# Self-attention of the sample streams in a hybrid streaming encoder: four 32-column tiles of the TensorE array, probabilities as the stationary operand

## The chip, the cores and the metric

The kernel runs on one core of one Trainium2 chip. The metric is the device time of one execution in microseconds (us), the median of three runs. A separate execution is recorded by the hardware profiler; every view of the profile below is of that one.

## The reference, cut to what matters

One inference layer of a chunk-causal encoder is computed for two groups of streams: a prompt of 2048 frames, and eight sample streams of 16 new frames each that carry 256 cached key and value rows. A layer is a mixer (banded attention with 8 heads of 64, beside a convolution module), a cross-attention into 256 memory tokens, and a feed-forward part, each with norms around it. The change touches only the banded attention of the samples:

```python
s = jnp.einsum("bqhd,bkhd->bhqk", qc, kc, preferred_element_type=jnp.float32) * scale + bias
s = jnp.where(valid[None, None, None, :], s, NEG_INF)
p = jax.nn.softmax(s, axis=-1)
return jnp.einsum("bhqk,bkhd->bqhd", p.astype(vc.dtype), vc)
```

For one sample the valid keys are its 256 cached rows and its own 16 new ones, 272 in all; there are 8 heads times 16 queries, so 128 rows of probabilities by 272 keys. All of it is float32.

## The kernel before, in words

The phases run one after the other in the program text: the memory keys and values, the input projection, the banded attention, the output projection of the mixer (`mixout`), cross-attention, gate and up, down. A planner of the language then orders the instructions of each engine by its own estimate of times and priorities, so that work of neighbouring phases and of different loop steps may stand mixed on an engine. Each engine then works off its list in that order.

`attention` walks over 128 units, one for each head and each block of 128 prompt queries. A unit makes scores (line 830), takes the softmax (lines 751 and 753), transposes the probabilities four steps later (line 847, four 128x128 transposes into a PSUM buffer of tag `t`, which ScalarE copies at line 848 and VectorE takes the remainder of at line 849) and multiplies by the values for four units at once (line 860, into the PSUM buffer of tag `o`, emptied at lines 864 and 866). The PSUM tags are `s` (two buffers of two banks), `t` (three buffers of one bank, given out in turn) and `o` (one buffer of one bank).

Beside the prompt runs one sample for each head: `sample(h)` is a generator, and the loop takes one step of it at every second unit (every unit in the first and last head, never at the first unit of a head). That gives seven steps in a head of the middle. The steps before the change:

- step 1 loads the sample's keys (line 758, on the SP queue) and values (lines 760 to 762, SP) and copies the new keys in (line 763, GpSimd). Steps 2 and 3 do nothing.
- step 4 fills `qb`, four blocks of 128 columns. Block c holds the queries of heads 2c and 2c+1, in 32 columns at the place 32c and zeros in the rest. Those zeros let four matmuls (line 776: 128 stationary columns, 272 moving) add up in one PSUM region to all 128 rows of scores. `qb` lies in two buffers of 128x640 words that are cleared once; because a block is written at a pitch of 160 words and read at one of 128, the place 32c comes about by itself. Softmax follows (lines 751, 753, 779, 780).
- step 5 transposes the probabilities in three blocks of 96, 96 and 80 keys (line 785, into a `t` buffer) and copies them to SBUF (lines 787 and 788, ScalarE), as `pp`.
- step 6 multiplies: for each of the four pairs of heads and each block of keys, the 128 value columns of the pair are stationary and the 32 probability columns move (line 794, 12 calls, into the `o` buffer). The result has channels on partitions, and VectorE copies the two halves that count into `attS` (lines 796 and 797). `mixout` reads `attS` for its first block.

A float32 matmul call of lines 776 and 794 stands in the trace as two weight loads and two matmuls: 4 calls a sample as 8 records at line 776, 12 calls as 24 at line 794. A transpose is one record a call.

Of the kernel before, what the change touches and what calls it, by code (L numbers as in the profile page):

```python
# [8 lines left out]
F32 = mybir.dt.float32  # L9
# [8 lines left out]
P = 128  # L18
# [12 lines left out]
DEC_S = 16  # L31
# [109 lines left out]
class Build:  # L141
# [591 lines left out]
    def attention(self):  # L733
        nc, A = self.nc, self.A
        sbF, sbR, ps, fa, fb = self.sbF, self.sbR, self.ps, self.fa, self.fb
        pool = (Region().lay(sbF, 34.5, ("kt", 4.25, 2), ("pp", 1.5, 1))
                .at("z", 2.5, (fa, [25, 22.5, 15, 20, 17.5]), (fb, [0, 2.5, 5]))
                .lay(sbF, 44.5, ("vc", 6, 1)).lay(fb, 7.5, ("vd", 6, 1)).lay(fb, 15.5, ("nmx", 0.03125, 12), ("sm", 0.03125, 2))
                .lay(fa, 0, ("qbd", 2.5, 2), ("otmp", 2, 1), ("bs", 1.0625, 1)).lay(fa, 10, ("bt", 2.5, 2))
                .at("q20", 8, (sbR, [0])).at("k20", 8, (sbR, [8])).at("kl0", 8, (sbR, [16])).at("v20", 8, (sbR, [72]))  # L740
                .at("q21", 8, (sbR, [24])).at("k21", 8, (sbR, [32])).at("kl1", 8, (sbR, [40])).at("v21", 8, (sbR, [80]))
                .lay(sbR, 48, ("ph0", 10, 1), ("pl0", 10, 1)).lay(sbR, 88, ("ph1", 10, 1), ("pl1", 10, 1)))
# [5 lines left out]
        def softmax_band(ps, w, bias, sm):  # L748
            z = self.t(pool, [P, W5], F32, "z", 6)
            nmx = self.t(pool, [P, 1], F32, "nmx", 12)  # L750
            nc.vector.tensor_tensor_reduce(out=z[:, :w], in0=ps, in1=bias, scale=-1.0, scalar=3e38,
                                           op0=ALU.add, op1=ALU.min, accum_out=nmx[:, :])
            nc.scalar.activation(z[:, :w], z[:, :w], AF.Exp, bias=nmx[:, :], scale=-1.0, accum_out=sm)
            return z

        def sample(s):
            kt = self.t(pool, [P, 4, PAST + DEC_S], F32, "kt")
            nc.sync.dma_start(kt[:, :, :PAST], A["cache_att_kT"][s])
            vc = self.t(pool, [KB, 3, 512], F32, "v" + "dc"[s % 2])
            nc.sync.dma_start(vc[:, :2, :], A["cache_att_v"][s, :2 * KB, :].rearrange("(b p) d -> p b d", p=KB))  # L760
            nc.sync.dma_start(vc[:KL - DEC_S, 2, :], A["cache_att_v"][s, 2 * KB:, :])
            nc.sync.dma_start(vc[KL - DEC_S:KL, 2, :], self.vsamp[s * DEC_S:(s + 1) * DEC_S, :])
            nc.gpsimd.tensor_copy(kt[:, :, PAST:], self.ksamp[:, :, s * DEC_S:(s + 1) * DEC_S])
            yield
            yield
            yield
            qb = qbds[s % 2]
            for o in range(2):
                rr = slice(o * DH, (o + 1) * DH)
                nc.vector.tensor_copy(qb[rr, :, o * DEC_S:(o + 1) * DEC_S],  # L770
                                      self.qsamp[rr, :, s * DEC_S:(s + 1) * DEC_S])
            qb = qb[:, :, :].rearrange("p c x -> p (c x)")
            n = PAST + DEC_S
            ps = self.t(ps_s, [P, 2, 512], F32, "s")[:, 0, :n]
            for c in range(4):
                nc.tensor.matmul(ps, qb[:, c * P:(c + 1) * P], kt[:, c, :], start=c == 0, stop=c == 3)
            sm = self.t(pool, [P, 1], F32, "sm", 2)
            z = softmax_band(ps, n, bs[:, :], sm[:, :])
            nc.vector.reciprocal(sm[:, :], sm[:, :])
            nc.gpsimd.tensor_scalar(z[:, :n], z[:, :n], sm[:, :], None, ALU.mult)  # L780
            yield
            pt = self.t(ps_t, [P, 3, P], F32, "t")
            blocks = [(b, KB if b < 2 else KL) for b in range(3)]
            for b, w in blocks:
                nc.tensor.transpose(pt[:w, b, :], z[:, b * KB:b * KB + w], self.ident[:, :])
            pp = self.t(pool, [KB, 3, P], F32, "pp", 1)
            nc.scalar.copy(pp[:, :2, :], pt[:KB, :2, :])
            nc.scalar.copy(pp[:KL, 2, :], pt[:KL, 2, :])
            yield
            po = self.t(ps_o, [P, 4, 32], F32, "o")  # L790
            for c in range(4):
                cc, hc = slice(c * P, (c + 1) * P), slice(c * 32, (c + 1) * 32)
                for b, w in blocks:
                    nc.tensor.matmul(po[:, c, :], vc[:w, b, cc], pp[:w, b, hc], start=b == 0, stop=b == 2)
            ss = slice(s * DEC_S, (s + 1) * DEC_S)
            nc.vector.tensor_copy(self.attS[:DH, :, ss], po[:DH, :, :DEC_S])
            nc.vector.tensor_copy(self.attS[DH:, :, ss], po[DH:, :, DEC_S:])
# [73 lines left out]
        bs = self.t(pool, [P, PAST + DEC_S], F32, "bs")  # L871
# [1 line left out]
            nc.sync.dma_start(bs[h * DEC_S:(h + 1) * DEC_S, :], toep[h][:DEC_S, PAST:2 * PAST + DEC_S])  # L873
        qbds = []
        for _ in range(2):
            qb = self.t(pool, [P, 4, P + 2 * DEC_S], F32, "qbd")
            nc.gpsimd.memset(qb[:, :, :], 0.0)
            qbds.append(qb)
        fill = iter(())
# [6 lines left out]
        for i in range(n + LV + 1):  # L886
            if i < n:
                h, t = units[i]
                if t == 0:
                    fill = sample(h)  # L890
                if t == 6 and h + 1 < H:
                    heads[h + 1] = load_head(h + 1)
                zq[h, t] = scores(heads[h], t, self.sums[:, t, h:h + 1])
            u = i - LT
            if 0 <= u < n:
                h, t = units[u]
                quads[u // 4] = transp({x: zq.get((h, x)) for x in range(t - t % 4, t + 1)}, t, quads.get(u // 4))
            u = i - LV
            if 0 <= u < n and u % 4 == 3:
                h, t = units[u]  # L900
                values(h, heads[h], t - 3, quads.pop(u // 4))
            if i < LATE:
                for _ in islice(late, 4 if i < LATE - 1 else None):
                    pass
            elif i % NPT and (i < NPT or i % 2 == 0 or i > SLAST):
                next(fill, None)
            if i == n - NPT:
                self.selectors()
            if i in WEIGH:
                for _ in self.weigh(WEIGH.index(i), ps_t, "t"):  # L910
                    pass
            if i in (n - 13, n - 11, n - 9, n - 7):
                next(self.wo_load)
# [785 lines left out]
```

## Time and profile before

| | us |
|---|---|
| median of three runs | 2955.26 |
| the three runs | 2954.59, 2955.26, 2962.31 |
| the profiled execution, its own time | 2962.86 |
| its span in the profile | 2960.8 |
| TensorE busy in the span | 2905.3 |
| VectorE, ScalarE, GpSimd busy | 2131.0, 1338.0, 1418.2 |
| first to last matmul of the samples (lines 776, 785, 794) | 632.5 to 862.2 |

In the views, PE is TensorE's matmuls, PEld its weight loads, DVE VectorE, ACT ScalarE, POOL GpSimd and SP the engine that issues most transfers. A row of a group ends with count, busy time, mean duration in ns, and the idle time of the engine before it with what ended it. The duration of a matmul is modelled and overlaps with the next one; what a matmul costs in a row of its kind is the distance between two starts. "128*128 128x272" means 128 rows and 128 columns of the array, and 272 moving columns on 128 partitions.

### The profile page before, as it was taken

What the parts mean: (1) busy time and instruction counts of PE and PEld (TensorE: products, weight loads), DVE (VectorE), ACT (ScalarE), POOL (GpSimd) and SP (SyncE); (2) the same over time, 40 slices, a digit from 0 to 9 for tenths busy, and PEclk for the clock granted to TensorE, in tenths of its full rate; (3) what the DMA queues carried; (4) which work ended last, traced back from release to release, by engine and by line L of the source; (5) the groups of instructions that cost most, each with busy time, mean ns of one, the idle gap of its engine ahead of it and who ended that gap; (6) DMA issues with size and microseconds to landing.
All of it is one profiled execution on the core that took longest, in us unless ns stands there. A gap on an engine that the chain in (4) does not pass through costs nothing.

```text
span 2960.8 us, 45532 instructions
## 1 busy us (share of the span) xinstructions
PE 2905.3 (98%) x16680; PEld 2670.8 (90%) x16680; DVE 2131.0 (72%) x3074; ACT 1338.0 (45%) x2631; POOL 1418.2 (48%) x1334
## 2 busy tenths in 40 slices
PE   9999999989999999999999999999999999999998
PEld 8999999989987887887879999999999999888787
DVE  6787895888875666344459888787888998546666
ACT  4435465678883445233334333433344444333433
POOL 1358496731113344144457555465656775424413
PEclk9999999999999999999999999999999999999999
DMA  8735253665535656133355333544334446756664
GB/s 287 243 129 187 95 166 112 220 212 174 200 125 177 212 201 200 57 114 109 123 173 193 135 123 128 194 163 149 141 132 158 149 142 212 236 169 213 224 224 147
DMA packets 201458, 499.53 MB, mean 169 GB/s; under 512 B 19801, under 2 KB 91361, under 8 KB 192394
## 3 DMA queue, kind: packets, MB, share of 16 engines
q1 hardware_dynamic: 186306, 427.01, 43.6%
q0 software_dynamic: 14928, 69.61, 6.3%
q8 instruction: 131, 2.15, 0.3%
q14 instruction: 93, 0.76, 0.1%
HBM read 365.45 MB, written 141.81 MB: 171 GB/s over the span
## 4 chain that ended last, share of the span: by engine, by line
PE 40%; DVE 3%; DMA 3%; POOL 3%; issue 2%; ACT 1%; SPq 0%; DVEq 0%; POOLq 0%; ACTq 0%
PE psb L292 13%; PE psb L290 13%; PE psb L291 13%; DMA sbf<-in_w_down_dram 1%; PE psb L298 1%; POOL sbf L1512 1%; DMA sbf<-x 1%; DVE sbr L1582 1%; PE psb L1367 1%; DVE sbr L1390 0%; POOL sbf L348 0%; DVE sbx L1390 0%; DMA sbf<-hn 0%; DVE sbf L365 0%; DMA hn<-sbf 0%
## 5 line engine op out<-in xcount | busy, mean ns | idle before, releaser
L290 PE MATMUL psb<-sbr 128*128 128x384 f32 (+3 forms) x2808 | 941.3, 336 | 6.0 <-DVE sbx L657 2.1
L291 PE MATMUL psb<-sbr 128*128 128x384 f32 (+3 forms) x2356 | 804.4, 342 | 0.3
L292 PE MATMUL psb<-sbr 128*128 128x512 f32 (+3 forms) x1848 | 633.4, 344 | 4.6 <-DVE sbr L1582 4.4
L290 PEld LDWEIGHTS psb<-sbr 128*128 128x128 f32 x2808 | 530.3, 189 | 36.6 <-ACT sbr L1581 4.0
L292 PE MATMUL psb<-sbr,sbx 128*128 128x384 f32 (+2 forms) x1484 | 476.2, 322 | 0.0
L291 PEld LDWEIGHTS psb<-sbr 128*128 128x128 f32 x2356 | 444.9, 189 | 27.0 <-DVE sbr L340 0.9
L292 PEld LDWEIGHTS psb<-sbr 128*128 128x128 f32 x1848 | 347.9, 189 | 36.2 <-DVE sbr L1582 9.5
L298 PE MATMUL psb<-sbr 128*128 128x512 f32 x1200 | 295.0, 396 | 5.2 <-DVE flexb L1033 2.8
L1390 DVE TENSOR_TENSOR sbr<-sbf,sbr 128x512 fp32r<-128x512 f32 x258 | 264.4, 1028 | 40.5 <-ACT sbr L1389 39.6
L1389 ACT CAST sbr<-sbf 128x512 fp32r<-128x512 f32 x258 | 159.2, 620 | 278.8 <-PE psb L291 229.1
L292 PEld LDWEIGHTS psb<-sbr,sbx 128*128 128x128 f32 x1484 | 280.6, 189 | 0.1
L298 PEld LDWEIGHTS psb<-sbr 128*128 128x128 f32 x1200 | 223.6, 190 | 52.9 <-DVE flexb L1033 3.2
L523 DVE SCALAR_TENSOR_TENSOR psb<-sbf,psb 128x768 f32<-128x768 f32 (+1 forms) x290 | 264.3, 911 | 6.2
L1582 DVE TENSOR_TENSOR sbr<-sbf,sbr 128x384 fp32r<-128x384 f32 (+2 forms) x242 | 166.0, 710 | 97.5 <-ACT sbr L1581 93.8
L285 POOL TENSOR_TENSOR sbx<-sbf,sbr 128x1024 fp32r<-128x1024 f32 (+1 forms) x62 | 154.4, 2493 | 77.9 <-ACT sbr L283 63.4
L1512 POOL TENSOR_TENSOR sbf<-sbf 128x512 f32<-128x512 f32 x77 | 108.5, 1413 | 168.5 <-DMA sbf<-in_w_down_dram 166.9
L1581 ACT CAST sbr<-sbf 128x384 fp32r<-128x384 f32 (+2 forms) x242 | 112.3, 483 | 168.6 <-PE psb L291 144.1
L533 POOL TENSOR_TENSOR flexb<-flexb,flexb 128x128 f32<-128x128 f32 (+1 forms) x180 | 168.5, 936 | 26.5 <-ACT flexb L532 17.9
L290 PE MATMUL psb<-sbr,sbx 128*128 128x384 f32 (+1 forms) x524 | 170.6, 327 | 0.7 <-ACT sbr L1369 0.7
L1389 ACT CAST sbx<-sbf 128x512 fp32r<-128x512 f32 x153 | 94.7, 620 | 161.4 <-PE psb L291 150.0
L1390 DVE TENSOR_TENSOR sbx<-sbf,sbx 128x512 fp32r<-128x512 f32 x153 | 154.0, 1008 | 14.9 <-ACT sbx L1389 14.6
L1384 POOL TENSOR_TENSOR sbf<-sbf 128x512 f32<-128x512 f32 x66 | 98.3, 1489 | 108.1 <-DVE sbr L1390 50.8
(327 smaller groups left out, 6129.6 us busy)
## 6 DMA issues: line engine op xcount, KB each, us to landing
af<-flexb SPq DMA_DIRECT2D x33, 1344.0 KB, 6.2
sbf<-in_w_down_dram SPq DMA_DIRECT2D x154, 256.0 KB, 3.7
sbf<-in_w_gate_dram SPq DMA_DIRECT2D x66, 512.0 KB, 3.4
sbf<-in_w_up_dram SPq DMA_DIRECT2D x66, 512.0 KB, 3.4
sbf<-af SPq DMA_DIRECT2D x85, 384.0 KB, 4.3
sbf<-x SPq DMA_DIRECT2D x49, 512.0 KB, 3.8
sbf<-in_w_in_dram SPq DMA_DIRECT2D x48, 512.0 KB, 3.9
sbr<-ks POOLq DMA_DIRECT2D x16, 1024.0 KB, 9.1
```

The lines of the kernel that those rows point to most:

```text
L285: self.lo_engine.tensor_tensor(lo[:, c], wf[:, c], hi[:, c].bitcast(F32), ALU.subtract)
L290: nc.tensor.matmul(ps, lh, rh, start=start, stop=False, **kw)
L291: nc.tensor.matmul(ps, lh, rl, start=False, stop=False, **kw)
L292: nc.tensor.matmul(ps, ll, rh, start=False, stop=stop, **kw)
L298: nc.tensor.matmul(y[o], l, r[:, o * 512:(o + 1) * 512], start=start and x == 0, stop=stop and x == 2)
L523: nc.vector.scalar_tensor_tensor(acc if w < CW - 1 else o, src(w), cwt[:, j, w:w + 1], acc, ALU.mult, ALU.add)
L533: nc.gpsimd.tensor_tensor(o, o, v, ALU.add)
L1389: nc.scalar.copy(hs[j][:, :], src[j])
L1390: nc.vector.tensor_tensor(ls[j][:, :], src[j], hs[j][:, :].bitcast(F32), ALU.subtract)
L1512: nc.gpsimd.tensor_tensor(acc[:, :], acc[:, :], q[:, :], ALU.add if s > 0 else ALU.subtract)
L1581: nc.scalar.copy(ch[:, m], a[:, x, m])
L1582: nc.vector.tensor_tensor(cl[:, m], a[:, x, m], ch[:, m].bitcast(F32), ALU.subtract)
```

## The change

The score matmuls now write only the 32 rows of their pair of heads. `qb` shrinks to 32 columns for each pair, without the zeros around them, and each of the four calls has a `tile_position` of (0, 32c): 32 columns of the array, with the other three calls on the other columns. Each starts and ends its own sum.

In the second product the operands change places: the 32 probability columns of a pair are stationary, on the same four column tiles, and the 128 value columns of the pair move. The loop over blocks of keys is now the outer one. The result, `px`, has the 128 head-and-query rows on partitions. VectorE copies it to SBUF (`ob`); one more step of the generator, the seventh, transposes it (128x128), and the two copies into `attS` follow from there. Both `px` and the transposed `po` lie in buffers of tag `t`; the samples no longer use `o`.

```diff
-                .lay(fa, 0, ("qbd", 2.5, 2), ("otmp", 2, 1), ("bs", 1.0625, 1)).lay(fa, 10, ("bt", 2.5, 2))
+                .lay(fa, 0, ("qbd", 0.5, 2), ("ob", 0.5, 2)).lay(fa, 5, ("otmp", 2, 1), ("bs", 1.0625, 1)).lay(fa, 10, ("bt", 2.5, 2))
...
-            qb = qb[:, :, :].rearrange("p c x -> p (c x)")
             n = PAST + DEC_S
             ps = self.t(ps_s, [P, 2, 512], F32, "s")[:, 0, :n]
             for c in range(4):
-                nc.tensor.matmul(ps, qb[:, c * P:(c + 1) * P], kt[:, c, :], start=c == 0, stop=c == 3)
+                nc.tensor.matmul(ps[c * 32:(c + 1) * 32], qb[:, c, :], kt[:, c, :], start=True, stop=True,
+                                 tile_position=(0, c * 32), skip_group_check=True)
...
             yield
-            po = self.t(ps_o, [P, 4, 32], F32, "o")
-            for c in range(4):
-                cc, hc = slice(c * P, (c + 1) * P), slice(c * 32, (c + 1) * 32)
-                for b, w in blocks:
-                    nc.tensor.matmul(po[:, c, :], vc[:w, b, cc], pp[:w, b, hc], start=b == 0, stop=b == 2)
+            px = self.t(ps_t, [P, P], F32, "t")
+            for b, w in blocks:
+                for c in range(4):
+                    cc, hc = slice(c * P, (c + 1) * P), slice(c * 32, (c + 1) * 32)
+                    nc.tensor.matmul(px[hc, :], pp[:w, b, hc], vc[:w, b, cc], start=b == 0, stop=b == 2,
+                                     tile_position=(0, c * 32), skip_group_check=True)
+            ob = self.t(pool, [P, P], F32, "ob")
+            nc.vector.tensor_copy(ob[:, :], px[:, :])
+            yield
+            po = self.t(ps_t, [P, 4, 32], F32, "t")
+            nc.tensor.transpose(po[:, :, :].rearrange("p c x -> p (c x)"), ob[:, :], self.ident[:, :])
             ss = slice(s * DEC_S, (s + 1) * DEC_S)
             nc.vector.tensor_copy(self.attS[:DH, :, ss], po[:DH, :, :DEC_S])
             nc.vector.tensor_copy(self.attS[DH:, :, ss], po[DH:, :, DEC_S:])
...
-            qb = self.t(pool, [P, 4, P + 2 * DEC_S], F32, "qbd")
+            qb = self.t(pool, [P, 4, 2 * DEC_S], F32, "qbd")
             nc.gpsimd.memset(qb[:, :, :], 0.0)
```

## The prediction

> **What bounds the kernel now.** First the page, then busy time by stretch in the stage where the samples run, then the matmul groups of that stage (630 to 870 us).
>
> ```profile
> span 2960.8 us, 45532 instructions
> PE 2905.3 (98%) x16680; PEld 2670.8 (90%) x16680; DVE 2131.0 (72%) x3074; ACT 1338.0 (45%) x2631; POOL 1418.2 (48%) x1334
> ```
> ```profile
> core 0: us, PE busy (x) PEld busy (x) DVE busy (x) ACT busy (x) POOL busy (x), PEclk, DMA share, GB/s
> 640.00:680.00 40.00, 39.52 (x278) 37.58 (x279) 33.84 (x80) 34.07 (x80) 5.02 (x9) 0.96 0.61 215
> 760.00:800.00 40.00, 39.63 (x282) 37.01 (x280) 33.69 (x85) 33.73 (x81) 5.53 (x11) 1.00 0.56 194
> ```
> ```profile
> L830 PE MATMUL psb<-sbr 128*128 128x384 f32 (+2 forms) x420 | 90.9, 340 | 2.9 <-DVE flexb L751 2.8
> L847 PE MATMUL psb<-ident,flexb 128*128 128x128 f32 x524 | 79.5, 278 | 1.0 <-DVE sbx L849 0.8
> L860 PE MATMUL psb<-sbx,sbr 128*128 128x128 f32 (+3 forms) x229 | 42.1, 327 | 0.9 <-DVE sbf L866 0.9
> L776 PE MATMUL psb<-sbf,flexb 128*128 128x272 f32 x64 | 17.6, 423 | 1.0 <-POOL flexb L308 1.0
> L794 PE MATMUL psb<-sbf 96*128 96x32 f32 (+1 forms) x96 | 12.0, 274 | 0.1
> L794 PE MATMUL psb<-sbf,flexb 96*128 96x32 f32 (+1 forms) x96 | 11.8, 274 | 0.3 <-ACT sbf L787 0.2
> ```
>
> TensorE has 39.6 of 40 us occupied; VectorE and ScalarE, next, have 34. Idle before the six groups is 6.2 us in 240 (2.9 + 1.0 + 0.9 + 1.0 + 0.1 + 0.3). Time taken from TensorE here is therefore time taken from the span, until VectorE's or ScalarE's 84% has become 100%, which is 6 us in 40 away. Everything after the stage moves forward with it.
>
> **What the samples' matmuls cost.** Two samples' rows at line 776, one's at line 794, all transposes of line 847 (ns: least, median, most), and a run of them from the timeline (start, length).
>
> ```profile
> L776 PE MATMUL psb<-sbf,flexb x8: 392/392/395, 700.6 to 702.2; 128*128 128x272 f32 x8
> L776 PE MATMUL psb<-sbf,flexb x8: 392/392/395, 731.2 to 732.8; 128*128 128x272 f32 x8
> ```
> ```profile
> L794 PE MATMUL psb<-sbf x24: 276/276/297, 859.6 to 862.2; 96*128 96x32 f32 x16, 80*128 80x32 f32 x8
> ```
> ```profile
> L847 PE MATMUL psb<-ident,flexb x560: 270/272/454, 636.1 to 888.1; 128*128 128x128 f32 x187
> ```
> ```profile
> 638.84 0.93 PE L847 MATMUL psb<-ident,flexb 128*128 128x128 f32 x7
> ```
>
> From first to last start, a score pass takes (702.2 - 700.6) / 7 = 0.229 us, a value pass (862.2 - 859.6) / 23 = 0.113. The transposes, 128 columns moving, go at (0.93 - 0.272) / 6 = 0.110. So a value pass of only 32 moving columns costs as much as one of 128: what it pays for is the load of 128 stationary columns. A sample costs 8 x 0.229 + 24 x 0.113 = 1.83 + 2.71 = 4.54 us, eight of them 36 us. That is all the change can work on.
>
> **The change, part by part.** (1) Array tiles. The number of passes stays at 8 and 24. After it, a value pass moves 128 columns against a load of 32, so alone it costs the transposes' 0.110; a score pass moves 272 columns as before, 0.229. The gain must come from passes on different columns going side by side, and no row of before shows two that do. The bounds: none side by side, 8 x 0.229 and 24 x 0.110 = 1.83 and 2.64 us; all four tiles side by side, 2 x 0.229 and 6 x 0.110 = 0.46 and 0.66 us. Between them stands an argument from the order. Each call is two passes on the same 32 columns, one right behind the other in the list (8 records for 4 calls). The second needs the columns that the first occupies, and if the list is not overtaken, the next call's first pass waits behind it. Then only the second pass of one call and the first of the next can share a slot: 4 calls take 5 slots, 12 calls take 13. I take that: 5 x 0.229 = 1.14 and 13 x 0.110 = 1.43, a gain of 0.69 + 1.28 = 1.97 us a sample.
>
> (2) Changing the array over. Nearest is line 982, where 16 rows of the array are used between matmuls on 128, against transposes in the same place:
>
> ```profile
> 878.22 0.61 PE L298 MATMUL psb<-sbr 128*128 128x512 f32 x2
> 878.76 0.66 PE L982 MATMUL psb<-sbr 16*128 16x128 f32 x4
> 879.35 0.50 PE L298 MATMUL psb<-sbr 128*128 128x512 f32 x1
> ```
> ```profile
> 874.00 0.62 PE L298 MATMUL psb<-sbr 128*128 128x512 f32 x2
> 874.46 0.60 PE L847 MATMUL psb<-ident,flexb 128*128 128x128 f32 x4
> 874.91 0.50 PE L298 MATMUL psb<-sbr 128*128 128x512 f32 x1
> ```
>
> Way in: 878.76 - 878.22 = 0.54 against 0.46. Way out: 879.35 - 878.76 = 0.59 against 0.45. Together 0.22 us for an excursion. The lower bound is 0, the upper that each change waits until the last pass has left the array, 0.272 - 0.110 = 0.16 each way, 0.32. I take 0.22. How many: the scores once; the values as often as the planner cuts them.
>
> ```profile
> 677.06 0.63 PE L794 MATMUL psb<-sbf 96*128 96x32 f32 x4
> 677.53 0.63 PE L847 MATMUL psb<-ident,flexb 128*128 128x128 f32 x4
> 678.00 2.22 PE L794 MATMUL psb<-sbf 80*128 80x32 f32 x18
> ```
>
> Now they are cut where the third block of keys is first needed, after 4 passes; with blocks outermost that comes after 16, so I count two pieces: three excursions, 0.66 us a sample. [...]
>
> (3) The transpose, one more pass: 0.11 us. (4) VectorE copies `px`, 128x128, then the two old copies follow. By form (VectorE, 636 to 890 us):
>
> ```profile
> L849 DVE TENSOR_TENSOR sbr<-psb,sbr 128x128 fp32r<-128x128 f32 x8 | 2.3, 282 | 0.0
> L796 DVE COPY sbf<-psb 64x64 f32<-64x64 f32 x8 | 1.7, 213 | 4.6 <-PE psb L794 4.6
> ```
>
> 0.28 us each, 2.3 in all, on an engine with 6 us free in 40. Its cover is TensorE's other work; without cover it would be 2.3 us. The copy makes VectorE wait for the product (as line 796 did, 4.6 us) and line 796 now for the transpose; behind it in VectorE's list stand lines 751 and 849, for which lines 830 and 847 wait. (5) `px` and `po` take two turns in the three `t` buffers, beside the transposes of line 847, which waited 1.0 us for a buffer in the stage. For (4) and (5) together I take 0.1 us a sample; bounds 0 and 0.28 + 0.1. The `o` buffer no longer has to serve both prompt and samples, which only helps.
>
> (6) Step 7 puts `attS` two units later. Its reader waits little, and the first matmul of `mixout` comes ten us later:
>
> ```profile
> 862.77 0.23 DVE L797 COPY sbf<-psb 64x64 f32<-64x64 f32 x1
> 873.46 0.47 PE L298 MATMUL psb<-sbr 128*128 128x512 f32 x1
> ```
>
> In the last head a step comes at every unit, about 2 us (a head of 16 units takes the 30.6 us from 700.6 to 731.2 between two samples' scores), so nothing is lost: the cover is some 8 us. Seven steps fit a head's seven turns. The SP queue holds the value loads of a later sample until line 794 has freed their buffer, so they come no later than now. The smaller `qb` shortens two clears on GpSimd, off the path: 0. (7) The planner will order the stage anew; by the 6.2 us of idle above, I bound that at -6 to +6 and take 0.
>
> (8) The clock. Twice the clock was halved right after a run of value passes, though TensorE was busy:
>
> ```profile
> 645.70:649.10 3.40, 3.40 (x31) 3.31 (x30) 3.40 (x9) 3.38 (x9) 0.00 (x0) 1.00 0.53 189
> 649.10:652.50 3.40, 3.40 (x17) 3.40 (x17) 1.99 (x7) 1.45 (x4) 0.89 (x2) 0.50 0.60 163
> 676.40:679.80 3.40, 3.29 (x30) 3.05 (x29) 3.37 (x8) 3.37 (x10) 0.00 (x0) 1.00 0.02 5
> 679.80:683.20 3.40, 3.40 (x16) 3.30 (x16) 1.70 (x5) 0.59 (x1) 0.00 (x0) 0.50 0.48 139
> 862.50:865.90 3.40, 3.40 (x27) 3.23 (x26) 2.17 (x5) 2.87 (x5) 0.00 (x0) 1.00 0.70 230
> ```
>
> Each dip is 3.4 us at half the clock, some 1.7 us lost. The other six samples had none (the last row follows the eighth). The passes ahead of the dips keep the array short of moving columns for 2.3 to 2.6 us of 3.4. After the change they last 1.43 us and move four times as many columns; that should end both dips, worth 3.4 us. I take one, 1.7, since what the clock gate counts on column tiles no row shows. [...]
>
> **The sum.** Each sample: -1.97 + 0.66 + 0.11 + 0.1 = -1.10; eight: -8.8; with the clock -10.5 us. The profiled execution took 2962.86 (span 2960.8 and 2.1 around it), 7.6 above the median of 2955.26, so a like one would take 2952.4; on the median, 2944.8, a gain of 0.36%. Its own range, with excursions at 0 to 0.32 us and the clock at 0 to 3.4, with (4) and (5) at 0 to 0.38, is -4 to -18: 2937 to 2951, the planner's 6 us not counted.
>
> **The rivals.** A: all four tiles side by side. Against it, the two passes of each call follow each other in the list; for it, nothing shows that the list can't be overtaken. Gain 1.37 + 2.05 = 3.42 a sample, less 0.87: 2.55 x 8 = 20.4, and both dips 3.4: 2931.5. [...] B: the change doesn't do what it says, no two passes overlap. Gain 0.07, cost 0.87: 0.80 x 8 = +6.4 us, dips as before: 2961.7. C, slower: on column tiles each pass waits until the one before has left the array, so a pass costs its whole duration, 0.392 and 0.276 us: 3.14 + 6.62 = 9.76 against 4.54, with 0.87 on top 6.1 x 8 = +49 us, 3004. It decides from the point where the 32 passes take more than (4.54 - 0.87) / 32 = 0.115 us each; against it, line 982's four matmuls kept a usual pace between the changes ((0.66 - 0.27) / 3 is 0.13, with the way in). D, slower: the clock gate counts the columns in use, a quarter of the array, so each of 16 bursts is followed by a dip: 14 more x 1.7 = 24, less the 8.8: +15, 2970. For it, two dips behind sparse passes; against it, bursts of 1.1 and 1.4 us fill less than half of a 3.4 us window.
>
> **How the numbers follow.** Forecast 0.40, A 0.18, B 0.22, C 0.08, D 0.12. About 0.3% (8.9 us) is what a measurement of this kernel can tell from no change. Faster by more than that, under 2946.4: 0.65 of the forecast's share, as its centre lies just beyond, and all of A: 0.44. Within: 0.14 of the forecast, 0.17 of B, 0.05 of D: 0.36. Slower, over 2964.1: 0.05 of B, 0.07 of D, all of C: 0.20. The range runs from A's 2931.5, a little widened, to just beyond B, 2930 to 2965: with a part of D it leaves out some 0.17.
>
> **What would show it.** The pace on the new score and value lines: 8 records in about 1.1 us and 24 in 1.4 mean pairs; 0.5 and 0.7 mean A; 1.8 and 2.6 mean B; starts 0.27 to 0.39 us apart mean C. The first start behind each burst shows the excursion. Clock rows of 0.50 behind the bursts show D, their absence the term (8). The copy of `px` should cost 0.28 us, with idle before lines 830 and 847 no larger than now. The prediction is wrong if the stage doesn't shorten by what the lines give up, or if time moves behind 875 us, where nothing of the change lies.

## The result, and the profile after

The changed kernel took 2935.45 us (median of four runs, 2931.87 to 2937.31) against 2958.78 for the kernel before on the same chip: ratio 0.9917, 95% interval 0.9904 to 0.993, some 24 us faster. On another chip it was 0.9943 (0.9927 to 0.996), 17 us. The forecast was -10.5 us, its own range 2937 to 2951; the range that was given, 2930 to 2965, holds the time because it was drawn to rival A's end. Rival A, all four tiles side by side, had -23.8. The profiled execution took 2931.87.

The page after, busy time by stretch in the stage of the samples, and the matmul groups of the stage (630 to 850 us; lines 830, 847 and 860 are now 836, 853 and 866):

```profile
span 2930.0 us, 45557 instructions
PE 2878.5 (98%) x16688; PEld 2641.6 (90%) x16688; DVE 2131.4 (73%) x3082; ACT 1339.1 (46%) x2631; POOL 1416.2 (48%) x1334
```
```profile
640.00:680.00 40.00, 39.40 (x321) 35.55 (x320) 36.07 (x90) 34.83 (x82) 5.53 (x11) 1.00 0.69 241
760.00:800.00 40.00, 39.80 (x315) 36.69 (x313) 37.43 (x91) 36.48 (x88) 3.88 (x9) 1.00 0.73 241
```
```profile
L836 PE MATMUL psb<-sbr 128*128 128x384 f32 (+2 forms) x420 | 89.1, 332 | 1.8 <-DVE flexb L751 1.6
L853 PE MATMUL psb<-ident,flexb 128*128 128x128 f32 x528 | 78.6, 276 | 1.0 <-DVE sbr L855 1.0
L866 PE MATMUL psb<-sbr 128*128 128x384 f32 (+3 forms) x176 | 36.3, 330 | 2.7 <-ACT sbr L854 1.7 <-DVE sbf L872 0.6 <-ACT sbr L283 0.4
L775 PE MATMUL psb<-sbf,flexb 128*32 128x272 f32 x64 | 5.8, 436 | 1.0 <-POOL flexb L308 1.0
L794 PE MATMUL psb<-sbf 96*32 96x128 f32 (+1 forms) x96 | 3.7, 278 | 0.0
L794 PE MATMUL psb<-flexb,sbf 96*32 96x128 f32 (+1 forms) x96 | 3.5, 277 | 0.0
```

The count of passes is the same (64 and twice 96), the time they cover has gone from 17.6 to 5.8 us and from 23.8 to 7.2. TensorE is as full as before; VectorE and ScalarE have moved from 34 of 40 us to 35 to 37, since the same work of theirs stands in less time. One sample's passes, and the timeline (start, length) around them:

```profile
L775 PE MATMUL psb<-sbf,flexb x8: 392/405/417, 663.1 to 663.4; 128*32 128x272 f32 x8
```
```profile
L794 PE MATMUL psb<-flexb,sbf x24: 270/273/298, 704.3 to 704.9; 96*32 96x128 f32 x16, 80*32 80x128 f32 x8
```
```profile
662.72 0.49 PE L853 MATMUL psb<-ident,flexb 128*128 128x128 f32 x3
663.14 0.67 PE L775 MATMUL psb<-sbf,flexb 128*32 128x272 f32 x8
663.74 0.50 PE L836 MATMUL psb<-sbr 128*128 128x256 f32 x2
```
```profile
703.85 0.56 PE L836 MATMUL psb<-sbr 128*128 128x128 f32 x3
704.34 0.86 PE L794 MATMUL psb<-flexb,sbf 96*32 96x128 f32 x24
705.13 0.50 PE L866 MATMUL psb<-sbx,sbr 128*128 128x512 f32 x1
```

Eight score passes start within 0.3 us, where eight in a row took 1.6, and 24 value passes within 0.6 instead of 2.6. From the score burst's start to the next matmul's are 663.74 - 663.14 = 0.60 us, from the value burst's 705.13 - 704.34 = 0.79.

How long a head takes, from the second sample's scores to the seventh's (five heads), of before and after:

```profile
L776 PE MATMUL psb<-sbf,flexb x8: 392/392/395, 668.2 to 669.8; 128*128 128x272 f32 x8
...
L776 PE MATMUL psb<-sbf,flexb x8: 392/392/395, 823.6 to 825.2; 128*128 128x272 f32 x8
```
```profile
L775 PE MATMUL psb<-sbf,flexb x8: 392/405/417, 663.1 to 663.4; 128*32 128x272 f32 x8
...
L775 PE MATMUL psb<-sbf,flexb x8: 392/405/417, 799.7 to 800.0; 128*32 128x272 f32 x8
```

(823.6 - 668.2) / 5 = 31.1 us before, (799.7 - 663.1) / 5 = 27.3 after. The five heads gain 18.8 us together. All seven heads between the first and the last sample's scores gain hardly more: 632.5 to 850.7, which is 218.2 us, against 629.4 to 828.2, 198.8, so 19.4 us.

### The profile page after: what moved, and what is told of

It reads as the page before. It is cut to its first block, busy times and chain, and to the rows that moved or that the text cites. A ratio compares the mean times of both kernels' runs of the same rounds, so it can differ in the third digit from the quotient of the medians.

```text
span 2930.0 us, 45557 instructions
## 1 busy us (share of the span) xinstructions
PE 2878.5 (98%) x16688; PEld 2641.6 (90%) x16688; DVE 2131.4 (73%) x3082; ACT 1339.1 (46%) x2631; POOL 1416.2 (48%) x1334
## 4 chain that ended last, share of the span: by engine, by line
PE 44%; DVE 3%; DMA 2%; POOL 1%; issue 1%; ACT 0%; SPq 0%; DVEq 0%; POOLq 0%; ACTq 0%
PE psb L292 14%; PE psb L291 14%; PE psb L290 14%; PE psb L298 1%; DMA sbf<-x 1%; PE psb L1373 1%; DMA sbf<-hn 0%; DVE sbr L1588 0%; DMA sbf<-in_w_gate_dram 0%; DVE sbr L1396 0%; DVE sbx L1396 0%; POOL sbf L348 0%; DMA hn<-sbf 0%; DVE flexb L1458 0%; DVE flexb L1460 0%
```

## The experiments

Two theories stood at the start. S: the passes go side by side on all four tiles. L: they only got cheaper because 32 stationary columns are loaded faster than 128 (0.11 us a load after, 0.19 before). All ratios are against the kernel before, in runs on the same chip; chips differ between some of the experiments. Where a diff names no other kernel, it starts from the changed one.

**Scores alone.** Only the first half of the change; the second product, its `o` buffer and six steps as before.

```diff
 (from the changed kernel)
-            px = self.t(ps_t, [P, P], F32, "t")
...
+            po = self.t(ps_o, [P, 4, 32], F32, "o")
+            for c in range(4):
+                cc, hc = slice(c * P, (c + 1) * P), slice(c * 32, (c + 1) * 32)
+                for b, w in blocks:
+                    nc.tensor.matmul(po[:, c, :], vc[:w, b, cc], pp[:w, b, hc], start=b == 0, stop=b == 2)
```

> The scores on four column tiles, the values and all behind them as before the change. Theory S (the tiles work side by side, four at once): a sample's scores take 0.69 us of TensorE with the change-over of the array instead of 1.84, so -1.15 x 8 = -9 us against before, ratio about 0.997; the value passes are still sparse, so a clock row of 0.50 behind some of them stays. Rival L (the gain lies in loading 32 stationary columns instead of 128, not in working side by side): the score passes were held by 272 moving columns and not by the load, so nothing is gained, ratio 1.000.

Measured: 0.9991 (0.9982 to 1.0001). The score calls are those of the changed kernel, where a sample's take 0.69 us with the change-over, and yet the time hardly moved. Stretches of 3.4 us show what stood against them: the old value passes start from 706.6 to 709.5 us, in the first, the clock is halved in the second, with TensorE busy throughout; the last row is behind the next sample's. (A row gives the stretch, its length, the busy time of PE, PEld, DVE, ACT and POOL, then clock, DMA share and GB/s.)

```profile
706.40:709.80 3.40, 3.40 (x33) 3.40 (x31) 2.46 (x6) 2.62 (x7) 0.00 (x0) 0.99 0.00 0
709.80:713.20 3.40, 3.40 (x17) 3.40 (x17) 2.45 (x10) 2.34 (x6) 1.74 (x3) 0.50 0.82 209
...
740.50:743.90 3.40, 3.40 (x17) 3.40 (x17) 1.85 (x6) 0.59 (x1) 0.91 (x2) 0.50 0.56 164
```

In this profile three halved stretches stand behind value passes, at 679, 709.8 and 740.5 us (clock 0.51, 0.50 and 0.50), where the kernel before had two. Two more places with a lower clock, 0.96 from 800 to 840 us and 0.87 from 840 to 880, come behind stretches in which TensorE waited:

```profile
825.80:829.20 3.40, 0.78 (x7) 0.57 (x5) 1.55 (x4) 3.19 (x6) 0.00 (x0) 1.00 0.00 0
856.50:859.90 3.40, 1.90 (x14) 1.16 (x12) 2.08 (x4) 3.40 (x7) 0.00 (x0) 1.00 0.00 0
```

Whether the clock or some other wait ate the gain was left to a run of its own below.

**Values alone.** The second half of the change, the scores as before (with the wide `qb`).

```diff
 (from the changed kernel)
-                nc.tensor.matmul(ps[c * 32:(c + 1) * 32], qb[:, c, :], kt[:, c, :], start=True, stop=True,
-                                 tile_position=(0, c * 32), skip_group_check=True)
+                nc.tensor.matmul(ps, qb[:, c * P:(c + 1) * P], kt[:, c, :], start=c == 0, stop=c == 3)
```

> The values on four column tiles with the copy, the seventh step and the transpose, the scores as before the change. Theory S: a sample's values take 0.89 us instead of 2.70, less 0.11 for the transpose, -1.70 x 8 = -13.6 us, and the clock dips behind the value passes go (-3): ratio about 0.9945. With the scores-only run the gains should add up to the whole change (0.9917). Rival L: all of the gain is here, ratio 0.992.

Measured: 0.9938 (0.9926 to 0.9951), as theory S had it; theory L's 0.992 lies outside. With the scores-only run that adds up to 0.9929, between the two measurements of the whole change.

**Tile by tile.** The two value loops exchanged.

```diff
-            for b, w in blocks:
-                for c in range(4):
+            for c in range(4):
+                for b, w in blocks:
```

> The changed kernel with the two value loops exchanged: all three blocks of keys of one tile, six passes, stand one behind the other, then the next tile. Theory S with overtaking (a pass whose columns are busy lets later ones by): 24 records in about 0.6 us as in the changed kernel, ratio 0.992. Theory S in order (the list isn't overtaken, and the two passes of a call only seemed to stand next to each other): only the borders between tiles overlap, 24 - 3 = 21 slots of 0.110 us = 2.3 us, +1.5 x 8 = 12 us against the changed kernel, ratio 0.996. Rival L: the order doesn't matter, 0.992.

Measured: 0.9942 (0.9929 to 0.9954), and in the trace:

```profile
L794 PE MATMUL psb<-flexb,sbf x24: 270/273/297, 710.0 to 711.3; 96*32 96x128 f32 x16, 80*32 80x128 f32 x8
```

By time alone it can't be told from the changed kernel (0.9917 and 0.9943). In the trace, 24 starts take 1.3 us: neither the 0.6 of a list that is freely overtaken nor the 2.3 of one that is not. The single starts show the pattern: the second tile's first pass comes 0.248 us after the first tile's, just when the first tile's third pass begins (0.242); the third and fourth tiles follow at the same distance, as the passes of the last block (80 rows) show, which start 0.460, 0.709, 0.957 and 1.206 us after the burst's first. With six passes to a tile, the first tile then had one running and three waiting; with two or four waiting, the next tile would have come with the first one's fourth or second pass, at 0.351 or 0.133 us. The middle way (one runs, three wait, one more holds up the list), the author's reading of these starts, gives 3 x 0.248 + 5 x 0.110 = 1.3 us from the first start to the last.

**One tile for all.** The value passes on one column tile, with the same loads.

```diff
-            px = self.t(ps_t, [P, P], F32, "t")
+            px = self.t(ps_t, [32, 4, P], F32, "t")
...
+                    nc.tensor.matmul(px[:, c, :], pp[:w, b, hc], vc[:w, b, cc], start=b == 0, stop=b == 2,
+                                     tile_position=(0, 0), skip_group_check=True)
...
+            for c in range(4):
+                nc.tensor.transpose(po[:, c, :], ob[:, c, :], self.ident[:32, :32])
```

> The changed kernel with all value passes on one and the same column tile: same passes, loads of 32 columns and 128 moving columns, results beside each other on 32 partitions, so a copy of 32x512 (about 0.68 us) and four transposes. Theory S: nothing can go side by side, 24 x 0.110 = 2.64 us plus 0.23 for the change-over, and 0.33 more for the transposes: +2.3 x 8 = 18 us against the changed kernel, ratio about 0.998. Rival L: the loads are as short as in the changed kernel, only the transposes and the copy are added, ratio 0.993.

Measured: 0.9993 (0.9984 to 1.0002).

```profile
L794 PE MATMUL psb<-flexb,sbf x24: 270/272/297, 710.5 to 713.0; 96*32 96x128 f32 x16, 80*32 80x128 f32 x8
```

(713.0 - 710.5) / 23 = 0.109 us a pass. With the loads just as short (0.109 us, 0.110 in the changed kernel) and the tiles taken away, the gain of the values is gone: theory L falls, and the 0.110 of the prediction's step (1) was right for a pass by itself. The time is some 4 us above the 0.998 that was expected; what took them was not followed.

This run also tells something of the clock. The burst uses 32 of the array's 128 columns for 2.5 us of a 3.4 us stretch, moves 128 columns a pass, and neither that stretch nor the next has less than the full clock, nor have the 135 us from 665 to 800 as a whole (1.00):

```profile
710.40:713.80 3.40, 3.40 (x29) 3.06 (x28) 2.34 (x7) 1.86 (x7) 1.14 (x2) 1.00 0.84 289
713.80:717.20 3.40, 3.40 (x28) 3.14 (x27) 1.75 (x7) 1.91 (x4) 0.00 (x0) 1.00 1.03 394
```

**Scores alone, with dense value passes.** The scores-only kernel with all 128 probability columns moving. Only the diagonal blocks are read.

```diff
 (from the scores-only kernel)
-            po = self.t(ps_o, [P, 4, 32], F32, "o")
+            po = self.t(ps_o, [P, 4, P], F32, "o")
...
-                    nc.tensor.matmul(po[:, c, :], vc[:w, b, cc], pp[:w, b, hc], start=b == 0, stop=b == 2)
+                    nc.tensor.matmul(po[:, c, :], vc[:w, b, cc], pp[:w, b, :], start=b == 0, stop=b == 2)
...
+                own = bass.AP(half.tensor, half.offset + o * DEC_S, [half.ap[0], [P + 32, 4], [1, DEC_S]])
+                nc.vector.tensor_copy(self.attS[o * DH:(o + 1) * DH, :, ss], own)
```

> The scores-only kernel with the old value passes moving all 128 probability columns instead of the 32 that count (the products that don't count are left unread): a pass is held by its load of 128 stationary columns either way, so TensorE's time stays at about 0.11 us a pass. Theory G (the gate halves the clock after a window of 3.41 us in which few columns move, however busy TensorE is, and that ate the scores' gain): no clock row of 0.50 behind value passes, and the -9 us that the scores save come through, ratio 0.9965. Rival W (the gain was lost in waits of other engines): dips or not, ratio stays at 0.999.

Measured: 0.9954 (0.9941 to 0.9968), clear of the 0.9991 of the same kernel with narrow passes (each against the kernel before on its own chip). The clock by stretch, of the run with narrow passes and of this one (the last columns are clock, DMA share, GB/s):

```profile
680.00:720.00 40.00, 40.00 (x282) 37.98 (x281) 32.80 (x81) 31.99 (x77) 5.53 (x11) 0.93 0.66 223
720.00:760.00 40.00, 39.42 (x284) 36.83 (x282) 32.99 (x80) 32.47 (x77) 4.63 (x11) 0.96 0.45 156
...
840.00:880.00 40.00, 38.40 (x224) 33.97 (x222) 30.49 (x73) 28.69 (x65) 10.72 (x5) 0.87 0.31 105
```
```profile
680.00:720.00 40.00, 40.00 (x298) 37.73 (x298) 35.05 (x86) 34.69 (x83) 4.66 (x12) 1.00 0.66 231
720.00:760.00 40.00, 39.17 (x291) 36.25 (x291) 35.28 (x88) 33.55 (x81) 5.57 (x11) 1.00 0.55 181
...
840.00:880.00 40.00, 37.47 (x241) 33.03 (x241) 30.25 (x58) 28.21 (x59) 9.80 (x6) 1.00 0.31 109
```

TensorE moves four times as many columns in its value passes (24 starts in 3.0 us, from 704.0 to 707.0, against 2.9 with narrow ones, from 706.6 to 709.5), is about as busy, and has 1.00 of its clock where it had 0.93 and 0.96. (The last pair of rows counts for less, since the drop in the run with narrow passes began behind a wait.) The granted clocks of all runs agree: on average 0.9914 for the scores-only kernel against 0.9938 for the kernel before beside it, 0.9942 against 0.9937 with dense passes. The 0.0024 that the first lost are 7 us of 2960, most of the 9 us that the scores should have gained. So the clock ate most of it; rival W, in which the ratio stays at 0.999, falls. How much of that clock was lost to the narrow passes themselves and how much behind waits isn't told apart.

**The kernel before, with dense value passes.** The same edit made to the kernel before, and nothing else.

> The kernel before with the same wider value passes and nothing else. Theory G: the dips behind value passes (two in the profile of before, 1.7 us each) are gone, other times unchanged, ratio 0.999 (0.9985 if other executions have three). Rival (the clock falls for the waits around the samples, not for the narrow passes): dips remain, ratio 1.000 or a little over, since 128 columns move where 32 did.

Measured: 0.9981 (0.9973 to 0.999): 5.6 us for an edit that adds work. The first sample's 24 value passes take 2.94 us, where they took 2.99 in the kernel before. No 40 us stretch from 640 to 840 us is below the full clock, where the same two stretches of before had 0.96. The granted clock of all runs rises from 0.9937 to 0.9954, which is 5 us of 2960, about the whole gain:

```profile
640.00:680.00 40.00, 39.41 (x289) 37.15 (x287) 35.06 (x83) 35.19 (x85) 5.04 (x9) 1.00 0.63 223
680.00:720.00 40.00, 39.96 (x294) 38.13 (x293) 33.80 (x84) 32.62 (x80) 5.58 (x11) 1.00 0.62 218
```

**Two blocks at a time.** A check on the middle way of the tile-by-tile run.

```diff
-            for b, w in blocks:
-                for c in range(4):
+            for c, b, w in [(c, b, w) for bs_ in (blocks[:2], blocks[2:]) for c in range(4) for b, w in bs_]:
```

> The changed kernel with the value calls in the order: blocks 1 and 2 of tile 0, of tile 1, of tile 2, of tile 3, then block 3 of each. Theory Q (passes are handed on in order, but one may run and three wait at a tile, so that only a fifth holds up the rest): four passes of a tile in a row hold nothing up, 24 starts within 0.6 us as in the changed kernel. Rival Q1 (one may wait): each tile begins two passes, 0.22 us, after the one before, 24 starts in about 1.2 us.

```profile
L794 PE MATMUL psb<-flexb,sbf x24: 270/273/298, 707.0 to 707.6; 96*32 96x128 f32 x16, 80*32 80x128 f32 x8
```

24 starts within 0.6 us with four passes of one tile in a row, 1.3 us with six. Theory Q agrees with both. The kernel was run only once (2943.33 us), so it has no ratio.

**No seventh step.** The `yield` behind the copy of `px` left out.

> The changed kernel without the added step: product, copy, transpose and the last copies in one step, left to the planner to fill. If the step is free as predicted (its cover is the last head's slack and other work), this is the same or slower: ratio 0.992 to 0.994, with TensorE waiting for the copy of px at up to 0.5 us a sample. If the longer life of attS and the later step cost something, it is faster: under 0.991.

Measured: 0.9933 (0.9919 to 0.9947), between the two measurements of the changed kernel, so the time alone tells nothing. By the trace the heads are longer:

```profile
L775 PE MATMUL psb<-sbf,flexb x8: 392/405/417, 664.2 to 664.5; 128*32 128x272 f32 x8
...
L775 PE MATMUL psb<-sbf,flexb x8: 392/405/417, 807.0 to 807.3; 128*32 128x272 f32 x8
```

(807.0 - 664.2) / 5 = 28.6 us against 27.3. That agrees with the step being of use and is no more than that.

**Query copies on GpSimd, and the changed kernel again.** In the first, the two copies into `qb` are made in step 1 on GpSimd.

```diff
-            yield
-            yield
-            yield
             qb = qbds[s % 2]
...
-                nc.vector.tensor_copy(qb[rr, :, o * DEC_S:(o + 1) * DEC_S],
+                nc.gpsimd.tensor_copy(qb[rr, :, o * DEC_S:(o + 1) * DEC_S],
...
+            yield
+            yield
+            yield
```

> The changed kernel with the two small copies into qb made on GpSimd in the sample's first step, beside the copy of the new keys, instead of on VectorE in step 4. In the changed kernel VectorE is busy 125 of 135 us in the stage. Theory V (VectorE is now close to being the bound): 0.38 us a sample off it shortens the stage by up to 3 us, 0.1%. Rival: TensorE is still the only bound there, no difference. Either way at the edge of what five rounds tell.

> The changed kernel once more, beside the run above: ratio 0.992 as the first time. It gives a second profile of it, in which no clock row of 0.50 should stand behind a sample's passes after the stage's first 30 us.

Measured: 0.993 (0.9917 to 0.9943) and 0.9943 (0.9927 to 0.996). The intervals overlap: whether VectorE binds by now isn't settled, and this is no better version that could be shown. The changed kernel was expected at 0.992 again and came out at 0.9943. Two of its six runs, 2953.23 and 2948.24 us, were granted a clock of 0.993 and 0.994, the other four, 2939.21 to 2944.87, had 0.995 to 0.996; where those two lost it, no profile shows. The second profile, of the fastest of the six, has the full clock from 640 us to the end of the stage, as expected.

## Why the prediction was right, and where it was too small

The prediction had the direction, what bounds the kernel and what the change can work on. It was luck that its range held: the overlap on which the forecast was built was wrong, and the range reached far enough because rival A was given its place.

**What bounds** was right: TensorE's passes were taken out of the span.

**Step (1), side by side, was the one that failed.** It took pairs, "if the list is not overtaken". The list is overtaken: in the tile-by-tile run the second tile's first pass started 0.248 us after the first tile's, when three of that tile's six had started; six passes of one tile in a row took 1.3 us for 24 starts, four in a row 0.6. The author reads that as one pass running and three waiting at a tile before the next tiles are held up. The change gives each tile two passes in turn, and all four tiles work together: four first passes start within 0.02 us, their second ones 0.253 us after them (scores) and 0.134 (values), 24 value passes in 0.594. That is 2 slots for the scores and 6 for the values, as in rival A, instead of 5 and 13. The term was to be -1.37 - 2.05 = -3.42 us a sample and was taken as -1.97. For the values the one-tile run shows that nothing but the tiles made it; for the scores the single starts do: the second pass on a tile comes 0.253 us after its first, no sooner than a pass of before (0.229). Rival B, no overlap, falls by the rows after the change, and so does C: passes start 0.006 to 0.233 us apart, not 0.27 to 0.39.

**Step (2), the change-over, was right in size and counted too often.** Three transposes at 0.11 us put the last start before the scores at 662.72 + 0.22 = 662.94; the first score pass comes 0.20 later, 0.09 more than a pass. On the way out, the last value pass starts at 704.94 and the next matmul at 705.13, again 0.19 later and 0.08 more than a pass. Within a burst the slots are a little longer than counted (0.594 us from the first value start to the last, where 5 x 0.110 is 0.55). All in all the scores take 0.60 + 0.09 = 0.69 us, which is 0.23 over two slots of 0.229, and the values 0.79 + 0.09 = 0.88, 0.22 over six of 0.110; 0.22 was taken. The values were cut in two only for one sample of eight, so there were 17 excursions, not 24.

**Steps (3) to (6).** The copy of `px` takes what its nearest row said:

```profile
L797 DVE COPY flexb<-psb x8: 273/282/292, 644.5 to 841.3; 128x128 f32<-128x128 f32 x8
```

The buffers of tag `t` cost nothing to be seen: idle before line 853 stayed at 1.0 us. The seventh step shows no cost: without it the heads were longer, 28.6 us against 27.3.

**Step (8), the clock, had the right cause; its size is less sure.** It allowed 3.4 us and took 1.7. The kernel before gains 5.6 (3 to 8), and has 1.00 of the clock where it had 0.96, when only the emptiness of its value passes is taken away, so 1.7 was too small. In the changed kernel no halved stretch stands in the stage from 640 us on, but what that is worth in its time can't be read so well: in the second measurement its granted clock is on average only 0.0005 above that of before, 1.4 us of 2960. One profile is a poor count of dips. Not every value burst brings one: in the first two of these rows of before, all 24 passes stand in one stretch (2.71 of its 3.40 us) and the next has its full clock (1.00); why is open. And dips come behind waits as well, as the last two rows show.

```profile
833.40:836.80 3.40, 3.40 (x33) 3.40 (x33) 2.41 (x7) 3.27 (x8) 0.00 (x0) 1.00 0.00 0
836.80:840.20 3.40, 3.40 (x26) 3.28 (x26) 2.83 (x7) 2.50 (x5) 1.57 (x1) 1.00 0.48 159
...
911.90:915.30 3.40, 0.91 (x5) 0.43 (x3) 1.62 (x5) 1.34 (x4) 0.94 (x3) 1.00 0.18 50
915.30:918.70 3.40, 3.11 (x7) 2.48 (x8) 0.89 (x2) 0.00 (x0) 2.37 (x1) 0.51 0.07 27
```

Rival D, a gate that counts array columns in use, falls by the one-tile run: there 2.5 us on a quarter of the array brought no dip. (The bursts of the changed kernel last 0.6 us, those ahead of the dips 2.3 to 2.6, so they say less.) The first dip of the kernel before lasts 3.41 us (the clock is 0.74 from 649.0 to 649.2 us, 0.50 after that, and 0.65 from 652.3 to 652.6, which puts the halved stretch at 649.10 to 652.51). That the clock is judged by stretches of this length, as the argument against D and theory G have it, no run shows.

**The sum.** With measured sizes: scores 1.83 less 0.69; values 2.71 less 0.88; a transpose of 0.11 more: -2.86 a sample, -22.9 for eight, and 5.6 for the clock make 28.5. Measured were 24 and 17. The profiles tell where the rest is. From the first score pass to the first matmul of `mixout` (line 298), in the kernel before and in the two profiles of the changed one:

```profile
632.46:873.46 241.00, 236.19 (x1654) 220.62 (x1655) 198.49 (x477) 199.52 (x461) 38.26 (x59) 0.98 0.52 182
629.39:847.59 218.20, 212.26 (x1644) 190.22 (x1645) 195.64 (x480) 195.61 (x456) 36.88 (x59) 0.99 0.59 202
630.24:847.08 216.84, 210.49 (x1644) 188.42 (x1645) 195.81 (x480) 195.57 (x457) 37.51 (x60) 1.00 0.60 203
```

The stage is 22.8 and 24.2 us shorter. The passes (22.9) and the two dips of this profile of before (3.4) make 26.3, so 2 to 4 us did not arrive. Step (7) had put the planner's new order at nothing, within 6 us; TensorE's idle time in the stage grew from 4.8 us to 5.9 and 6.4, above all before the value products of the prompt: 2.7 us at line 866, most of it until ScalarE's copy of line 854, against 0.9 at the same line before (860). VectorE, at 36 to 37 of 40 us, may bind as well; the run that moved its small copies away couldn't tell, and that stays open.

What is left of the difference doesn't show in the stage of these profiles. Behind it the kernel before took 2960.8 - 873.5 = 2087.3 us, the changed one 2082.4 and 2090.3, though nothing of the change lies there: 5 less and 3 more. The prediction had named time moving there as a sign of being wrong; it moves both ways, by about as much as the two measurements differ (24 and 17), so it tells neither for nor against the change.

## What to carry to other kernels

When a product has four independent parts of 32 stationary columns, try them on four column tiles and issue them in turn, tile after tile: here 24 passes started within 0.6 us instead of 2.6, for a change-over of 0.2 us a burst. Four passes of one tile in a row left the 24 starts at 0.6 us; six cost 0.7 us of the 1.9 that the values gained. And where a pass with few moving columns takes as long as one with many, let more columns move, even useless ones: 128 instead of 32 cost no time here (2.94 us for 24 passes, 2.99 before), and the clock was 1.00 instead of 0.96.

## What the hardware showed unexpectedly

- **Behind passes with few moving columns the clock was halved while TensorE was busy.** Widening the value passes from 32 to 128 moving columns, at the same pace (2.94 and 2.99 us for 24 of them), was worth 5.6 us in the kernel before, and turned 0.9991 into 0.9954 in the scores-only kernel. The halved stretch of the scores-only run (clock 0.50) follows one in which TensorE was busy for 3.40 of 3.40 us. The dip at 915.3 us of the kernel before (0.51) does follow a wait (busy 0.91 of 3.40). What exactly brings a dip is not shown: one burst of before, all 24 passes in one stretch (2.71 of 3.40 us), brought none.
- **Passes on other column tiles overtook, up to a limit.** The starts of the tile-by-tile burst interleave: the second tile's first pass came 0.248 us after the first tile's, 0.006 us after that tile's third. With six passes of a tile in a row the 24 starts took 1.3 us, against 0.6 with at most four.
- **A burst on column tiles added only its change-over to its slots**, 0.22 to 0.23 us, and that is what line 982's 16-row matmuls, a different shape of tile, had shown (0.22).
